# Attention scores of two maps as three 64-row products, one map in each half of the PE rows

## The chip, the cores and the metric

The kernel runs on one core of a Trainium2 chip. The metric is the device time of one execution in microseconds; lower is better. It is compared with the kernel before, run on the same chip.

## What is computed

One layer of an encoder on 1024 tokens of width 1024 in float32: a half-step SwiGLU feed-forward, a mixer, a second half-step feed-forward, each followed by a residual sum and a LayerNorm. Only the mixer is touched. It has two groups of heads:

```
differential attention, 4 heads, two maps m per head, head width 64:
  s[m] = q[m] . k[m] * scale + alibi         128 queries x 1024 keys at a time
  a    = softmax(s[0]) - lam * softmax(s[1]);   o = rms_norm(a . v)
neighbourhood attention, 8 heads of width 64, taken two at a time:
  s    = q . k * scale + bias                128 queries x a window of 264 to 384 keys
  o    = softmax(s) . v
```

So everywhere there are two score maps side by side (two maps of a head, or two heads), each a product over 64 numbers.

## The kernel before

Products are made in a float32 replacement: every operand is split in a rounded part "hi" and a remainder "lo" (fp32r), and a product is a sum of hi.hi, hi.lo and lo.hi.

`project` (L579) makes K and Q of one group of heads from the layer's input: for each half of the tokens 24 matmuls for K (L593 to L595), a split of the sum in PSUM into hi and lo (L606 on ACT, L607 on DVE), then 24 matmuls and a split for Q (L618 ACT, L619 DVE). It is a generator: each step issues three matmuls, and the attention code calls `fill()` at chosen places, which makes a step or two for the next group of heads. These matmuls fill PE while others wait.

The sum in PSUM has map 0 in partitions 0 to 63 and map 1 in 64 to 127. Before, each map gets a tile slice of all 128 partitions: `K[:, j]` holds hi of map j in that map's own half of the partitions and lo in the other half, so L606 and L607 are run once per map on 64 partitions. `Q[:, j, 0]` holds hi of map j in both halves, `Q[:, j, 1]` lo in both; the second half is made by a DMA (L620). One 128-row matmul with Q hi then gives hi.hi + hi.lo, one with Q lo gives lo.hi + lo.lo: two matmuls per map and piece of keys.

`df_scores` (L677) serves 32 units (4 heads, 8 query blocks). For map 1, then map 0: 4 matmuls of 512 columns (L688) into one PSUM tile of `psA` (two slots), a DVE pass that adds the ALiBi table and finds the row minimum (L691), an exponential on ACT (L694). `df_rest` transposes the result (L706), splits it (L708 ACT, L709 DVE) and for every second unit multiplies with V (L715); the tail of that (L724 to L738) goes through ACT, POOL and PE again.

`na_scores` (L814) serves 32 units (4 pairs of heads, 2 row halves, 4 column groups): both heads' scores lie in one `psA` tile, one PSUM bank each. For each head j: 2 matmuls (L825), a DVE pass (L829), an exponential (L831). Then transposes (L850), copies (L851, L852), and the product with V (L858), in which head j writes PSUM partitions 64j to 64j + 63 only, so that the array is used in column halves of 64.

What sets the order on each engine is not the source text: the framework plans a list schedule at compile time. An instruction that the plan finds ready early may go ahead of others that stand before it in the text, and the order on an engine is then fixed. So a unit's score matmuls come out in one or several pieces with other matmuls between them.

Of the kernel before, what the change touches and what calls it, by code (L numbers as in the profile page):

```python
# [9 lines left out]
FT = mybir.dt.float32  # L10
FR = mybir.dt.float32r
FH = mybir.dt.float16
BF = mybir.dt.bfloat16
AF = mybir.ActivationFunctionType
OP = mybir.AluOpType
# [6 lines left out]
P = 128  # L22
S = 1024
# [21 lines left out]
def tile_hybrid_layer(ctx: ExitStack, tc: tile.TileContext, I: dict, out: bass.AP, dbg=None):  # L45
    nc = tc.nc
    V, A, G, T = nc.vector, nc.scalar, nc.gpsimd, nc.tensor
    dma = nc.sync.dma_start
# [4 lines left out]
    psA = ctx.enter_context(tc.tile_pool(name="psA", bufs=2, space=PSUM))  # L53
# [14 lines left out]
    def split_w(src, pool=wsp, tag="wsp", eng=G):  # L68
        st = wst.tile([P, 1024], FT, name="wst")
        dma(st, src)  # L70
        sp = pool.tile([P, 2, 1024], FR, name=tag)
        split(sp[:, 0], sp[:, 1], st, eng)
        return sp
# [9 lines left out]
    def xk(t, k):  # L83
        x = xq[t][k // 4]
        return x[:, 0, k % 4], x[:, 1, k % 4]
# [460 lines left out]
    with ExitStack() as es:  # L546
# [4 lines left out]
        for i in range(2):  # L551
            for tb in range(8):
                o = slice(tb % 4 * P, tb % 4 * P + P)
                ps = psB.tile([P, 512], FT, name="psB")
                terms = []
                for k in range(KT):
                    w, cs = wv[i][k // 2], slice(k % 2 * 512, k % 2 * 512 + 512)
                    hi, lo = xk(tb // 4, k)
# [13 lines left out]
    with ExitStack() as es:  # L572
        kp = es.enter_context(tc.tile_pool(name="kp", bufs=2))
        qp = es.enter_context(tc.tile_pool(name="qp", bufs=3))
# [4 lines left out]
        def project(g):  # L579

            h, na = g["h"], g["kind"] == "na"
            cq, ck = (h, 4 + h) if na else (12 + h, 16 + h)
            scale = -0.125 if na else -0.125 / SLOPES[h]
            wk, wq = (split_w(I["w_in"][c]) for c in (ck, cq))
            K = g["K"] = kp.tile([P, 2, S], FR, name="K")
            g["Q"] = []

            def mm(w, t):
                ps = psB.tile([P, 512], FT, name="psB")
                for k in range(KT):  # L590
                    hi, lo = w[:, 0, k * P:(k + 1) * P], w[:, 1, k * P:(k + 1) * P]
                    xh, xl = xk(t, k)
                    T.matmul(ps, hi, xh, start=k == 0, stop=False)  # L593
                    T.matmul(ps, hi, xl, start=False, stop=False)  # L594
                    T.matmul(ps, lo, xh, start=False, stop=k == KT - 1)  # L595
                    if k < KT - 1:
                        yield ps
                yield ps

            for t in range(2):  # L600
                ts = slice(t * 512, (t + 1) * 512)
                for ps in mm(wk, t):
                    yield
                for j in range(2):
                    a, b = slice(64 * j, 64 * j + 64), slice(64 - 64 * j, 128 - 64 * j)
                    A.activation(K[a, j, ts], ps[a], AF.Copy, scale=scale)  # L606
                    V.scalar_tensor_tensor(K[b, j, ts], ps[a], scale, K[a, j, ts].bitcast(FT), OP.mult, OP.subtract)  # L607
                Q = qp.tile([P, 2, 2, 512], FR, name="Q")
                g["Q"].append(Q)
                for ps in mm(wq, t):  # L610
                    yield
                for j in range(2):
                    a, b = slice(64 * j, 64 * j + 64), slice(64 - 64 * j, 128 - 64 * j)
                    qi, hi, lo = ps[a], Q[a, j, 0], Q[a, j, 1]
                    if na:
                        qi = qi.rearrange("p (r c w) -> p c r w", c=4, w=16)
                        hi, lo = (x.rearrange("p (c r w) -> p c r w", c=4, w=16) for x in (hi, lo))
                    A.copy(hi, qi)  # L618
                    V.tensor_tensor(lo, qi, hi.bitcast(FT), OP.subtract)  # L619
                    dma(Q[b, j].bitcast(FT), Q[a, j].bitcast(FT))  # L620

        PIECES = 32
        groups = [dict(kind="df", h=h) for h in range(4)] + [dict(kind="na", h=h) for h in range(4)]
# [1 line left out]
        def filler(i, places):  # L625
            return Filler(project(groups[i]) if i < 8 else nothing(), PIECES, places)

        for _ in project(groups[0]):
            pass
# [33 lines left out]
        with ExitStack() as e2:  # L663
# [13 lines left out]
            def df_scores(g, qb):  # L677
                slope = SLOPES[g["h"]]
                Q, qo = g["Q"][qb // 4], (qb % 4) * P
                st = sm.tile([P, 8], FT, name="st")  # L680
                mn, bi, z, rz = st[:, 0:2], st[:, 2:4], st[:, 4:6], st[:, 6:8]
                off = 896 - qb * P
                e = [None, None]
                for j in (1, 0):
                    ps = psA.tile([P, S], FT, name="psA")
                    for kc in range(2):
                        for i in range(2):
                            T.matmul(ps[:, kc * 512:(kc + 1) * 512], Q[:, j, i, qo:qo + P],  # L688
                                     g["K"][:, j, kc * 512:(kc + 1) * 512], start=i == 0, stop=i == 1)
                    ej = e[j] = ep.tile([P, S], FT, name="e")  # L690
                    V.tensor_tensor_reduce(ej, ps, dist[:, off:off + S], 1.0, 3e38, OP.add, OP.min,  # L691
                                           accum_out=mn[:, j:j + 1])
                    V.tensor_scalar(bi[:, j:j + 1], mn[:, j:j + 1], slope, None, OP.mult)
                    A.activation(ej, ej, AF.Exp, bias=bi[:, j:j + 1], scale=-slope,  # L694
                                 accum_out=z[:, j:j + 1])
                V.reciprocal(rz, z)
                V.scalar_tensor_tensor(rz[:, 1:2], z[:, 0:1], nlam, rz[:, 1:2], OP.mult, OP.mult)
                V.scalar_tensor_tensor(e[0], e[1], rz[:, 1:2], e[0], OP.mult, OP.add)
                return e[0], rz[:, 0:1]
# [59 lines left out]
            for i, (g, qb) in enumerate(units):  # L759
                if qb == 0 and i:  # L760
                    fill.drain()
                    fill = filler(i // 8 + 1, 24)
                queue.append((g, qb, df_scores(g, qb)))
                if tail:
                    tail.pop()()
                fill()
                if qb == 0:
                    load_v(g)
                if len(queue) > 1:
                    df_rest()  # L770
# [11 lines left out]
        with ExitStack() as e2:  # L782
# [31 lines left out]
            def na_scores(g, r, c, tabs):  # L814
                (r0, nr), (c0, nc_, kind) = NA_R[r], NA_C[c]
                nk = nr * nc_
                t0 = nr * sum(x[0] for x in NA_KINDS[:kind])
                Kg = g["K"].rearrange("p m (r c) -> p m r c", c=GW)
                ps = psA.tile([P, 2, 512], FT, name="psA")
                st = sm.tile([P, 8], FT, name="st")  # L820
                mn, z, rz = st[:, 0:2], st[:, 2:4], st[:, 4:6]
                es_ = []
                for j in range(2):
                    for i in range(2):
                        T.matmul(ps[:, j, 0:nk], g["Q"][r][:, j, i, c * P:(c + 1) * P],  # L825
                                 Kg[:, j, r0:r0 + nr, c0:c0 + nc_], start=i == 0, stop=i == 1)
                    e = pp.tile([P, 384], FT, name="pe")
                    es_.append(e)
                    V.tensor_tensor_reduce(e[:, 0:nk], ps[:, j, 0:nk], tabs[j][:, t0:t0 + nk],  # L829
                                           1.0, 3e38, OP.add, OP.min, accum_out=mn[:, j:j + 1])  # L830
                    A.activation(e[:, 0:nk], e[:, 0:nk], AF.Exp, bias=mn[:, j:j + 1], scale=-1.0,  # L831
                                 accum_out=z[:, j:j + 1])
                V.reciprocal(rz, z)
                for j in range(2):
                    G.tensor_scalar(es_[j][:, 0:nk], es_[j][:, 0:nk], rz[:, j:j + 1], ones, OP.mult, OP.mult)
                return es_
# [58 lines left out]
            for i in range(4, 8):  # L895
                g = groups[i]
# [133 lines left out]
```

## Time and profile before

| | us |
|---|---|
| median of 3 runs (lowest, highest) | 1953.94 (1952.79, 1955.36) |
| the profiled execution | 1954.6 |
| span of its instructions | 1952.8 |
| its part outside the span | 1.8 |
| mixer, differential heads, from 775 to 1013 us | 238 |
| mixer, neighbourhood heads, from 1013 to 1190 us | 177 |

The views name engines as PE (TensorE matmuls), PEld (its weight loads), DVE, ACT, POOL and SP. A matmul's duration contains its way through the array, so that neighbours overlap; what one costs in a row of them is the distance from start to start.

### The profile page before, as it was taken

To read this page: it belongs to the slowest core of one execution; us is meant where nothing else is said; L and a number is where in the kernel's file an instruction comes from. 1 tells how busy PE (TensorE), PEld (TensorE's weight loads), DVE (VectorE), ACT (ScalarE), POOL (GpSimd) and SP (SyncE) were. 2 spreads that over 40 slices of the span, in tenths; PEclk is the share of its full clock that TensorE was granted. 3 is DMA by queue.
4 is the path that set the end of the run, shared out by engine and by line. 5 is a ranking of instruction groups with operands and counts; after the bars stand their busy time and mean duration, and the time that the engine had idled before them with its cause. 6 is when DMAs were issued, how large, how long until landed. Compare 5 with 4: busy or idle time off the path is not lost. (4 is left out here: it accounts for less than half of the span.)

```text
span 1952.8 us, 24037 instructions
## 1 busy us (share of the span) xinstructions
PE 1911.4 (98%) x9056; PEld 1549.9 (79%) x9056; DVE 1205.7 (62%) x1807; ACT 752.5 (39%) x1196; POOL 211.4 (11%) x188
## 2 busy tenths in 40 slices
PE   9999999999999999999999998999999999999998
PEld 7777888878888888788887776887777888878887
DVE  8575656546556811888875455787666555555557
ACT  5333333335332222566655454133333333344331
POOL 0000000000001330011116443100000000000005
PEclk9999999999999999999999999999999999999999
DMA  4656322248762263122123336124554222378632
GB/s 169 217 198 225 119 103 114 108 163 314 250 194 98 103 209 94 43 62 70 47 52 79 90 114 218 74 88 162 195 204 183 102 83 101 134 281 286 194 119 86
DMA packets 109843, 280.41 MB, mean 144 GB/s; under 512 B 12320, under 2 KB 31648, under 8 KB 102048
## 3 DMA queue, kind: packets, MB, share of 16 engines
q1 hardware_dynamic: 109728, 278.89, 41.7%
q8 instruction: 71, 1.16, 0.2%
q14 instruction: 44, 0.36, 0.1%
HBM read 191.29 MB, written 79.17 MB: 138 GB/s over the span
## 5 line engine op out<-in xcount | busy, mean ns | idle before, releaser
L79 PE MATMUL psA<-s,wsp 128*128 128x512 f32 x480 | 189.6, 395 | 0.0
L79 PE MATMUL psA<-x,wsp 128*128 128x512 f32 x448 | 180.7, 403 | 7.7 <-ACT t L378 5.9
L81 PE MATMUL psA<-s,wsp 128*128 128x512 f32 x480 | 187.4, 390 | 0.0
L80 PE MATMUL psA<-s,wsp 128*128 128x512 f32 x480 | 186.7, 389 | 0.0
L65 ACT CAST wsp<-wr 128x1024 fp32r<-128x1024 f32 x124 | 128.9, 1049 | 128.4 <-DVE wr L206 121.3
L80 PE MATMUL psA<-x,wsp 128*128 128x512 f32 x448 | 175.7, 392 | 0.8 <-DVE x L66 0.6
L81 PE MATMUL psA<-x,wsp 128*128 128x512 f32 x448 | 174.9, 390 | 0.0
L66 DVE TENSOR_TENSOR wsp<-wr,wsp 128x1024 fp32r<-128x1024 f32 x124 | 149.4, 1222 | 12.1 <-ACT wsp L65 12.1
L66 DVE TENSOR_TENSOR hd<-wst,hd 128x1024 fp32r<-128x1024 f32 x84 | 101.9, 1224 | 76.3 <-ACT hd L65 73.0
L66 POOL TENSOR_TENSOR wsp<-wst,wsp 128x1024 fp32r<-128x1024 f32 x24 | 60.8, 2538 | 774.2 <-ACT wsp L65 774.2
L205 DVE TENSOR_TENSOR wr<-wr 128x1024 f32<-128x1024 f32 x40 | 49.0, 1224 | 148.5 <-DMA wr<-in_wgu 148.3
L65 ACT CAST hd<-wst 128x1024 fp32r<-128x1024 f32 x84 | 87.7, 1053 | 124.6 <-PE psA L435 31.6
L65 ACT CAST wsp<-wst 128x1024 fp32r<-128x1024 f32 (+1 forms) x86 | 88.7, 1032 | 97.7 <-DMA wst<-wTd 20.7
L79 PEld LDWEIGHTS psA<-x,wsp 128*128 128x128 f32 x448 | 84.0, 187 | 44.0 <-ACT t L378 17.3
L435 PE MATMUL psA<-hd 128*128 128x512 f32 x504 | 116.2, 389 | 0.0
L66 DVE TENSOR_TENSOR wsp<-wst,wsp 128x1024 fp32r<-128x1024 f32 (+1 forms) x62 | 73.6, 1190 | 63.4 <-ACT wsp L65 57.6
L145 POOL TENSOR_TENSOR mv<-mv,cols 128x1 f32<-128x1 f32 x24 | 35.5, 1479 | 712.9 <-DVE mv L144 712.9
L79 PEld LDWEIGHTS psA<-s,wsp 128*128 128x128 f32 x480 | 90.0, 188 | 25.4 <-ACT sg L395 8.2
L435 PEld LDWEIGHTS psA<-hd 128*128 128x128 f32 x504 | 94.6, 188 | 19.6
L593 PE MATMUL psB<-x,wsp 128*128 128x512 f32 x256 | 107.1, 418 | 0.0
L81 PEld LDWEIGHTS psA<-s,wsp 128*128 128x128 f32 x480 | 90.1, 188 | 19.7
L80 PEld LDWEIGHTS psA<-s,wsp 128*128 128x128 f32 x480 | 90.2, 188 | 17.9
(185 smaller groups left out, 4231.0 us busy)
## 6 DMA issues: line engine op xcount, KB each, us to landing
wr<-in_wgu SPq DMA_DIRECT2D x42, 1024.0 KB
hSd<-hs SPq DMA_DIRECT2D x18, 1792.0 KB
wst<-hSd SPq DMA_DIRECT2D x126, 256.0 KB
wst<-wTd SPq DMA_DIRECT2D x72, 256.0 KB
wst<-in_wd SPq DMA_DIRECT2D x54, 256.0 KB
wt<-in_wd SPq DMA_DIRECT2D x18, 512.0 KB
wt<-in_wd SPq DMA_DIRECT2D x36, 256.0 KB
wTd<-wt SPq DMA_DIRECT2D x36, 256.0 KB
```

Of the source, the lines that this page charges most:

```text
L65: A.copy(hi, x)
L66: eng.tensor_tensor(lo, x, hi.bitcast(FT), OP.subtract)
L79: T.matmul(ps, ah, bh, start=start and j == 0, stop=False, skip_group_check=skip)
L80: T.matmul(ps, ah, bl, start=False, stop=False, skip_group_check=skip)
L81: T.matmul(ps, al, bh, start=False, stop=j == n - 1, skip_group_check=skip)
L145: G.tensor_tensor(mv[:, 3:4], mv[:, 2:3], mhalf[:, 0:1], OP.pow)
L205: V.tensor_tensor(l[:, 0:4:3], l[:, 2:4], l[:, 3:5], OP.subtract)
L435: T.matmul(banks[T_], o[:, x, a], o[:, w, 512:1024], start=start and p == 0 and j == 0, stop=p == NP - 1 and j == 2, skip_group_check=not ...
L593: T.matmul(ps, hi, xh, start=k == 0, stop=False)
```

## The change

K and Q are kept once, each map in its own half of the partitions, hi and lo beside each other. The splits run on all 128 partitions at once, the DMA that doubled Q is gone, and lo.lo is left out. A score is three matmuls of 64 rows (hi.hi, hi.lo, lo.hi); those of map 0 and map 1 are issued in turns, with operands in partitions 0 to 63 and 64 to 127. In `df_scores` both PSUM tiles are taken first and all 12 matmuls stand ahead of the first DVE pass; in `na_scores` all 6 stand ahead of it.

```diff
-                for j in range(2):
-                    a, b = slice(64 * j, 64 * j + 64), slice(64 - 64 * j, 128 - 64 * j)
-                    A.activation(K[a, j, ts], ps[a], AF.Copy, scale=scale)
-                    V.scalar_tensor_tensor(K[b, j, ts], ps[a], scale, K[a, j, ts].bitcast(FT), OP.mult, OP.subtract)
-                Q = qp.tile([P, 2, 2, 512], FR, name="Q")
+                A.activation(K[:, 0, ts], ps, AF.Copy, scale=scale)
+                V.scalar_tensor_tensor(K[:, 1, ts], ps, scale, K[:, 0, ts].bitcast(FT), OP.mult, OP.subtract)
+                Q = qp.tile([P, 2, 512], FR, name="Q")
...
-                    A.copy(hi, qi)
-                    V.tensor_tensor(lo, qi, hi.bitcast(FT), OP.subtract)
-                    dma(Q[b, j].bitcast(FT), Q[a, j].bitcast(FT))
+                A.copy(hi, qi)
+                V.tensor_tensor(lo, qi, hi.bitcast(FT), OP.subtract)
...
+                pss = [psA.tile([P, S], FT, name="psA") for _ in range(2)]
+                for kc in range(2):
+                    for i, (x, y) in enumerate(((0, 0), (0, 1), (1, 0))):
+                        for j in range(2):
+                            a = slice(64 * j, 64 * j + 64)
+                            T.matmul(pss[j][:, kc * 512:(kc + 1) * 512], Q[a, x, qo:qo + P],
+                                     g["K"][a, y, kc * 512:(kc + 1) * 512], start=i == 0, stop=i == 2)
                 for j in (1, 0):
-                    ps = psA.tile([P, S], FT, name="psA")
-                    for kc in range(2):
-                        for i in range(2):
-                            T.matmul(ps[:, kc * 512:(kc + 1) * 512], Q[:, j, i, qo:qo + P],
-                                     g["K"][:, j, kc * 512:(kc + 1) * 512], start=i == 0, stop=i == 1)
+                    ps = pss[j]
...
+                for i, (x, y) in enumerate(((0, 0), (0, 1), (1, 0))):
+                    for j in range(2):
+                        a = slice(64 * j, 64 * j + 64)
+                        T.matmul(ps[:, j, 0:nk], g["Q"][r][a, x, c * P:(c + 1) * P],
+                                 Kg[a, y, r0:r0 + nr, c0:c0 + nc_], start=i == 0, stop=i == 2)
                 for j in range(2):
-                    for i in range(2):
-                        T.matmul(ps[:, j, 0:nk], g["Q"][r][:, j, i, c * P:(c + 1) * P],
-                                 Kg[:, j, r0:r0 + nr, c0:c0 + nc_], start=i == 0, stop=i == 1)
```

## Rows read from the trace of the kernel before

**Rows 1.** The page, part 1: busy time, share of the span, instructions.
```profile
PE 1911.4 (98%) x9056; PEld 1549.9 (79%) x9056; DVE 1205.7 (62%) x1807; ACT 752.5 (39%) x1196; POOL 211.4 (11%) x188
```
**Rows 2.** Busy time by stage: stretch, its length, engines in the columns' order PE, PEld, DVE, ACT, POOL.
```profile
775.00:1013.00 238.00, 229.43 (x1300) 190.57 (x1299) 199.24 (x430) 149.97 (x297) 31.63 (x23) 1.00 0.20 55
1013.00:1190.00 177.00, 166.50 (x1032) 127.48 (x1033) 91.56 (x284) 96.64 (x265) 89.22 (x115) 0.97 0.35 97
```
**Rows 3.** Groups by line, 700 to 1340 us: the score matmuls (busy, mean ns | idle before).
```profile
L688 PE MATMUL psA<-K,Q 128*128 128x512 f32 x256 | 72.1, 399 | 0.4 <-DVE st L691 0.4
L825 PE MATMUL psA<-K,Q 128*128 128x384 f32 (+3 forms) x128 | 34.8, 358 | 6.2 <-DVE st L829 6.1
```
**Rows 4.** Timeline of PE, one differential unit: start us, length us.
```profile
802.20 1.98 PE L688 MATMUL psA<-K,Q 128*128 128x512 f32 x8
804.01 0.39 PE L593 MATMUL psB<-x,wsp 128*128 128x512 f32 x1
```
**Rows 5.** Timelines of PE and DVE, one neighbourhood unit.
```profile
1088.11 0.42 PE L825 MATMUL psA<-K,Q 128*128 128x288 f32 x2
1088.36 0.39 PE L593 MATMUL psB<-x,wsp 128*128 128x512 f32 x1
...
1088.83 0.40 PE L595 MATMUL psB<-x,wsp 128*128 128x512 f32 x1
1089.19 0.53 PE L825 MATMUL psA<-K,Q 128*128 128x288 f32 x2
1089.57 0.39 PE L593 MATMUL psB<-x,wsp 128*128 128x512 f32 x1
...
1089.06 0.08 DVE L829 DVE_READ_ACCUMULATOR2_ANT st<- 128x1 f32 x1
```
**Rows 6.** Waits from 1013 to 1190 us: total us, times, longest.
```profile
PEld psA L825 <- DVE st L829: 13.5, 22, 3.2
...
PE psA L825 <- DVE st L829: 6.1, 5, 2.7
```
**Rows 7.** Timelines of PE and PEld around one product with V in column halves.
```profile
1054.84 0.40 PE L595 MATMUL psB<-x,wsp 128*128 128x512 f32 x1
1055.16 1.15 PE L858 MATMUL psB<-PT,Vc 128*64 128x128 f32 x12
...
1056.04 0.27 PE L858 MATMUL psB<-PT,Vc 96*64 96x128 f32 x1
1056.24 0.50 PE L593 MATMUL psB<-x,wsp 128*128 128x512 f32 x1
1056.58 0.40 PE L594 MATMUL psB<-x,wsp 128*128 128x512 f32 x1
...
1056.24 0.19 PEld L593 LDWEIGHTS psB<-x,wsp 128*128 128x128 f32 x1 [0.17 <-issue]
```
**Rows 8.** PE's L858 matmuls begun up to two instants of that product (stretch, busy, count).
```profile
1055.10:1055.44 0.34, 0.27 (x3) 1.00 0.30 76
1055.10:1055.82 0.72, 0.65 (x9) 1.00 0.30 75
```
**Rows 9.** Timeline of PE: first and last piece of L688 (71) and of L825 (61).
```profile
775.76 1.98 PE L688 MATMUL psA<-K,Q 128*128 128x512 f32 x8
...
1011.40 0.63 PE L688 MATMUL psA<-K,Q 128*128 128x512 f32 x2
1011.87 1.47 PE L715 MATMUL psB<-aT,Vt 128*128 128x256 f32 x11
1013.17 0.41 PE L825 MATMUL psA<-K,Q 128*128 128x264 f32 x2
...
1183.55 0.54 PE L825 MATMUL psA<-K,Q 128*128 128x288 f32 x2
```
**Rows 10.** Groups by line, 700 to 1340 us: splits of 64 and of 128 partitions.
```profile
L709 DVE TENSOR_TENSOR aT<-psB,aT 128x512 fp32r<-128x512 f32 x64 | 43.3, 685 | 3.2 <-ACT aT L708 3.0
...
L708 ACT CAST aT<-psB 128x512 fp32r<-128x512 f32 x64 | 35.5, 584 | 19.3 <-PE psB L706 18.9
...
L607 DVE SCALAR_TENSOR_TENSOR K<-psB,K 64x512 fp32r<-64x512 f32 x32 | 22.0, 688 | 51.0 <-ACT K L606 50.3
...
L606 ACT ACTIVATE K<-psB 64x512 fp32r<-64x512 f32 x32 | 18.9, 589 | 20.4 <-PE psB L595 10.9 <-DVE K L607 9.1
```

## Prediction before the run

> **What bounds the kernel now.** I read the page's busy shares first: PE is busy 98% of the span and no other engine over 62% [rows 1]. A share of the whole says little about the stage that is changed, so the windows by stage come next: with the differential heads PE is busy 229.4 of 238 us and DVE 199.2; with the neighbourhood heads PE 166.5 of 177 and DVE only 91.6 [rows 2]. PE ends both stages: its idle time is 8.6 and 10.5 us, and its order is fixed, so a microsecond more or less of PE work moves the end by nearly as much. The granted clock is 1.00 and 0.97 there, so PE time can be read at the upper level. The groups by line give the size of what is changed: 256 score matmuls of 512 columns and 128 of 264 to 384 (mean 322) [rows 3]. Their mean durations overlap; the price comes from the timeline: eight L688 from 802.20 to the next matmul at 804.01 are 0.227 us each [rows 4], and two L825 of 288 columns take 0.25 [rows 5], 0.125 each, or some 0.14 at 322.
>
> **The change, part by part.** One execution is the base: 1954.6 us, of which 1952.8 are span; the median of the runs is 1953.94, 0.7 less. About 0.2% (4 us) is what a measurement of this kernel can tell from no change.
>
> *Matmuls.* A differential unit had 8 and gets 12 of half the rows. The trace has no matmul of 64 rows. It does have halves of the array's columns, in L858: three of them start in the first stretch of a product, before the second head joins, then six within 0.38 us [rows 8], 63 ns each, although within one column half they follow each other at 109 ns (of the twelve the last three start between 1055.82 and 1056.04, two such distances [rows 7, 8]). So two halves of the array do work at once in this kernel. For row halves the bounds are 0.227 us per pair (both at once) and 0.454 (one after the other). I take 0.227, as the row of the nearest kind shows overlap. Six pairs replace eight matmuls: 2 x 0.227 x 32 units = 14.5 us less. A neighbourhood unit goes from 4 to 3 slots: 32 x 0.14 = 4.5 us less.
>
> *Entering and leaving the halves.* This is the price that decides, and again L858 is the nearest row. From L595 to the first L858 it is 0.325 us instead of 0.227: 0.10 lost, and the weight load that usually hides behind a matmul starts only then. On the way out the last L858 starts at 1056.04 and would be followed 0.109 later; L593 comes at 1056.24, its weight load marked with 0.17 us in which it waited for nothing visible, and L594 follows after 0.34 instead of 0.227 [rows 7]. So out is 0.09 of emptying plus 0.11 of exposed load; in is 0.10 plus the same 0.11 for a 128-column load. One visit costs 0.41 us, near the 0.454 that a unit saves. Bounds: 0 (row halves switch freely) and 0.41; I take 0.41, since all the trace's changes between whole array and halves pay it. The Trainium skill (TensorEngine Tiling (Array Packing), Key Properties) says that changing the tiling mode, not merely the tile, drains TensorE. The trace agrees for column halves with the 0.17 us above; no run here shows it for row halves. By that rule the sum is the one below; without it the first rival's.
>
> *How many visits.* The plan breaks a unit's scores in pieces: L688 stands in 71 pieces for 32 units, from one of eight to one of two with L715 behind it; L825 in 61 [rows 9]. For the differential heads I take two per unit, 64, with ends at 32 (each unit in one piece) and 85 (longer lists are broken more). 64 x 0.41 = 26.2 us. A piece with an odd count leaves one half empty for a slot: half of the pieces x 0.114 = 3.6 us. Differential heads: -14.5 + 26.2 + 3.6 = +15.3.
>
> For the neighbourhood heads the two pieces per unit have a cause: the second L825 pair starts at 1089.19, right after DVE has read the first head's scores at 1089.14 [rows 5]; they share a tile. Waits of L825 for that read are 13.5 us on the load side and 6.1 on the matmul side [rows 6]. The change puts all six matmuls ahead of the read, so this wait goes; I take 7 us, between 3 (the 2.7 and 2.2 us stalls are those of a late bias table and of the last heads without filler, and may return at the transposes) and 10. With the cause gone I expect 1.25 pieces per unit, 40 visits (ends 32 and 61): 16.4 us. 18 of the 122 borders of L825 pieces lie against L858, which already pays one border: 18 x 0.2 = 3.6 less. Odd pieces 0.6. Neighbourhood heads: -4.5 - 7 + 16.4 - 3.6 + 0.6 = +1.9.
>
> *Splits, DMAs and passes.* A split costs the same on 64 and 128 partitions (688 and 685 ns on DVE, 589 and 584 on ACT) [rows 10], so half of 64 go on each: 22 us off DVE, 19 off ACT, over eight groups of heads. 32 DMAs of 256 KB leave SP's queue, with nothing moved past it. All of that lies beside PE's filler matmuls; what it can give is a part of PE's 8.6 us idle time. I take 1 us, between 0 and 4. The DVE pass of map 1 now stands behind all 12 matmuls instead of 4, some 0.5 to 1 us later; its readers come an iteration later and PE has other matmuls meanwhile: nothing. If that cover were gone, as with the last unit of a stage, 1 us once. The first matmul needs both PSUM slots instead of one; in steady units they are free when the scores come, and where not, the plan puts filler first: inside the count of pieces.
>
> **Sum.** +15.3 + 1.9 - 1 = +16.2: 1954.6 + 16.2 = 1970.8, said as 1971. This case alone reaches from 32 + 32 visits with the larger wait and no odd pieces (-1.4 - 5.0 - 3 = about -9: 1946) to 85 + 61 visits with the smaller wait (+25.2 + 15.0 = +40: 1995).
>
> **Rivals.**
> 1. *Row halves switch freely.* Its place is the border between L595 and L688, its price 0 instead of 0.41; it decides below some 0.2 us per visit, where the sum changes sign. Then -14.5 + 3.6 with the differential heads, -4.5 - 7 + 0.6 with the others, -1: -23, 1932. For it: row halves leave the way to PSUM as wide as it was, other than column halves. Against it: the border costs of L858 are the same whatever stands beside it. 16%.
> 2. *The halves take turns.* Pairs at 0.454 us: with the differential heads 128 x 0.227 = +29 instead of -14.5, and visits +26.2; with the others 64 x 0.14 = +9 instead of -4.5, waits and visits as above +5.8; -1: +69, odd pieces costing nothing here: 2024. It decides as soon as a pair takes over 0.3 us. For it: no row shows row halves at work; against it: column halves overlap [rows 8]. The Trainium skill (TensorE: Matmul & The Clock Gate, Part 3) reports four row tiles at 3.07 times the speed of one after the other; no run here shows that. 12%.
> 3. *The plan keeps each unit in one piece.* 32 + 32 visits: differential -14.5 + 13.1 = -1.4, neighbourhood -4.5 - 7 + 13.1 - 3.6 = -2, -1: about -4 to -9, 1948. For it: the differential lists are longer, so that PE is fuller in the plan; against it: 71 pieces now. 9%.
> 4. *Nothing measurable*, where PE's idle time takes up what the visits add: 5%. Against it: the idle time lies at other places.
>
> **How the numbers follow.** My case has 58%. Its middle is slower; of its spread some 0.05 falls within 4 us and 0.02 below. Faster: 0.16 + 0.08 of rival 3 + 0.02 = 0.26, with a little of rival 4 0.27. Same: 0.05 + 0.04 = 0.09. Slower: the rest of mine and rival 2, 0.64. The range goes from 1930, so that most of rival 1 is in, to 2000, the end of mine and a little; outside lie rival 2 and an edge of rival 1, under 2 in 10. My own case's range is 1946 to 1995.
>
> **What would show it.** In the timeline after: starts of the two halves' matmuls in pairs a few ns apart, and 0.22 to 0.24 us from pair to pair (rival 2: 0.45). From L595 to the first score matmul 0.32 or more, and a score piece followed by a weight load with about 0.17 us of unexplained idle time; rival 1 has neither. The pieces of L688's successor counted: some 64, and 40 with the neighbourhood heads. The wait of the scores for L829 gone. The stage from 775 grows by about 15 us, the next by 2. I am wrong if the first stage shrinks, or if PE's busy time there grows while its end stays.

## The result, and the profile after

The kernel after takes 1984.9 us (median of five runs, 1977.17 to 1986.13) against 1953.94 before: 1.0144 times the time, with an interval of 1.0127 to 1.016. That is 31 us more, inside the range and on the side that was forecast, but nearly twice the 16.2 us of the sum. The profiled execution took 1985.38 us, 1983.6 of it span.

The page's busy shares say little, as before [rows 1]: PE gained 23 us of busy time and the span 31.

```profile
PE 1934.2 (98%) x9248; PEld 1542.1 (78%) x9248; DVE 1184.7 (60%) x1775; ACT 731.3 (37%) x1164; POOL 209.2 (11%) x188
```

The windows by stage show where the time went (columns as in [rows 2]). The stage from 775 us to the first neighbourhood scores now ends at 1054 instead of 1013, with 21.9 us in which PE is idle instead of 8.6, and at a mean clock of 0.98; the next one is 9 us shorter.

```profile
775.00:1054.00 279.00, 257.10 (x1465) 191.98 (x1464) 197.49 (x427) 144.47 (x291) 31.91 (x24) 0.98 0.11 34
1054.00:1222.00 168.00, 161.05 (x1042) 117.26 (x1041) 72.50 (x257) 81.25 (x240) 86.99 (x113) 0.95 0.25 73
```

Work of the two stages overlaps at their border, so from here on I cut at the last tail transposes of the differential heads (L735, before L737), and call what lies from the first score matmul to there the differential stage, and from there to the last product with V the neighbourhood stage. By that cut, in one profiled execution of each kernel, the change adds 34.5 us to the first (252.6 to 287.1) and takes 3.4 from the second (164.3 to 160.9). The rest of the program is unchanged.

The groups by line (700 to 1360 us) stand beside [rows 3] and [rows 10]: 384 score matmuls of 64 rows in place of 256, 192 in place of 128, and a split that takes 0.69 us on 128 partitions as it did on 64. The scores' wait for the DVE pass fell from 6.1 us to 2.4.

```profile
L684 PE MATMUL psA<-K,Q 64*128 64x512 f32 x384 | 69.3, 421 | 0.0
L824 PE MATMUL psA<-K,Q 64*128 64x264 f32 (+3 forms) x192 | 26.9, 368 | 2.6 <-DVE st L829 2.4
L605 DVE SCALAR_TENSOR_TENSOR K<-psB,K 128x512 fp32r<-128x512 f32 x16 | 11.0, 689 | 50.0 <-ACT K L604 50.0
```

What had grown is in the waits from 775 to 1054 us (total us, times, longest). On the matmul side the tail transposes L735 wait 15.8 us for the end of their chain, where the corresponding wait of before (L737, from 775 to 1013 us, the second view) is 4.4 in five. On the load side there is a row that stands for the visits themselves: the first score load of a piece waits, 32 times, for nothing visible, and so does L593 behind a piece, 17 times.

```profile
PEld psB L735 <- issue: 20.9, 13, 3.5
PE psB L735 <- DVE rr L730: 15.8, 11, 3.1
...
PEld psA L684 <- issue: 8.9, 32, 0.4
...
PEld psB L593 <- issue: 6.2, 17, 0.4
PE psB L704 <- DVE e L696: 5.0, 9, 1.0
```

```profile
PE psB L737 <- DVE rr L732: 4.4, 5, 0.9
```

One of the long tail waits, on PE (timeline: start, length). Twelve score matmuls end near 885, and the next instruction in PE's order is the tail's transpose, 3.06 us later.

```profile
883.06 0.40 PE L595 MATMUL psB<-x,wsp 128*128 128x512 f32 x1
883.39 1.65 PE L684 MATMUL psA<-K,Q 64*128 64x512 f32 x12
888.10 0.66 PE L735 MATMUL psB<-ident,rr 128*128 128x128 f32 x2 [3.06 <-DVE rr L730]
888.41 0.77 PE L593 MATMUL psB<-x,wsp 128*128 128x512 f32 x1
888.98 0.63 PE L594 MATMUL psB<-x,wsp 128*128 128x512 f32 x1
```

Behind the wait the first two filler matmuls stand 0.57 us apart (888.41 to 888.98); behind another tail of the same trace, at full speed, it is 0.32 (868.54 to 868.86). The windows show why: the granted clock is 1.00 up to 887 and 0.51, the 1.2 GHz level, for the next 7 us. Two more of the three long waits (near 957 and 1028 us) are followed by such stretches. From 775 to 1217 us the time at the lower level adds up to 30.7 us after and 13.6 before; a microsecond of PE work costs two there. Of the 30.7 us after, 13.7 lie in the differential stage and 17.0 in the other, near 1075 and 1206 us.

```profile
880.00:887.00 7.00, 5.04 (x37) 3.83 (x35) 4.42 (x5) 3.28 (x9) 2.35 (x1) 1.00 0.00 0
887.00:894.00 7.00, 5.90 (x22) 4.59 (x24) 4.42 (x11) 2.80 (x5) 0.69 (x1) 0.51 0.32 94
```

### The profile page after: what moved, and what is told of

The parts are those of the page before. It is cut to its first block, busy times and chain, and to the rows that moved or that the text cites. A ratio compares the mean times of both kernels' runs of the same rounds, so it can differ in the third digit from the quotient of the medians.

```text
span 1983.6 us, 24174 instructions
## 1 busy us (share of the span) xinstructions
PE 1934.2 (98%) x9248; PEld 1542.1 (78%) x9248; DVE 1184.7 (60%) x1775; ACT 731.3 (37%) x1164; POOL 209.2 (11%) x188
## 5 line engine op out<-in xcount | busy, mean ns | idle before, releaser
L65 ACT CAST wsp<-wr 128x1024 fp32r<-128x1024 f32 x124 | 129.0, 1050 | 128.3 <-DVE wr L206 121.4
L66 DVE TENSOR_TENSOR wsp<-wr,wsp 128x1024 fp32r<-128x1024 f32 x124 | 149.4, 1223 | 12.0 <-ACT wsp L65 12.0
L66 DVE TENSOR_TENSOR hd<-wst,hd 128x1024 fp32r<-128x1024 f32 x84 | 101.9, 1223 | 76.5 <-ACT hd L65 73.2
L66 POOL TENSOR_TENSOR wsp<-wst,wsp 128x1024 fp32r<-128x1024 f32 x24 | 57.8, 2410 | 805.8 <-ACT wsp L65 805.7
L65 ACT CAST hd<-wst 128x1024 fp32r<-128x1024 f32 x84 | 87.8, 1054 | 124.6 <-PE psA L435 28.8
L65 ACT CAST wsp<-wst 128x1024 fp32r<-128x1024 f32 (+1 forms) x86 | 88.8, 1033 | 99.5 <-PE psB L435 20.0
L593 PE MATMUL psB<-x,wsp 128*128 128x512 f32 x256 | 113.3, 443 | 0.0
L66 DVE TENSOR_TENSOR wsp<-wst,wsp 128x1024 fp32r<-128x1024 f32 (+1 forms) x62 | 73.8, 1190 | 62.7 <-ACT wsp L65 58.3
```

The costliest lines, as they stand in the source:

```text
L65: A.copy(hi, x)
L66: eng.tensor_tensor(lo, x, hi.bitcast(FT), OP.subtract)
```

## The experiments

The theory after the traces: the half rows do what the sum said (work in pairs, a fixed price per visit), and two things were not in it, the new order of the matmuls and the tail waits. The rival: the price of a visit is larger than 0.41 us and explains all.

### What a visit costs, by itself

In place of the layer (which is left out, the output is the input) a row of matmuls: six of the whole array, then some in halves, again and again.

> This kernel leaves the whole layer out: its output is the input, and it only runs rows of matmuls of one kind behind each other, so that their prices can be read from start to start. Theory (each visit to row halves is paid on the way in and out, the halves work at once): a pair of 64-row matmuls 0.23 us in a long row; a visit of six pairs between whole matmuls 6 x 0.23 + 0.41 us; a visit of one pair 0.23 + 0.41; a visit of a single 64-row matmul the same as that of one pair; a long row in one half alone 0.23 each. Rival (halves switch freely and the loss after the change came from the plan): a visit of six pairs 1.4 us, of one pair 0.25. For six matmuls in one half and then six in the other I have no firm number: between 1.4 us (the queue reaches past six) and 2.8 us plus the visit.

Timeline of PE of that kernel: six whole ones and a visit of six pairs; of one pair (L77); long rows of 64 in turns and of 32 in one half; six in one half and then six in the other (L91); six halves of 288 columns (L96) and four whole ones (L101).

```profile
36.98 1.65 PE L70 MATMUL full<-w 128*128 128x512 f32 x6
38.57 1.66 PE L72 MATMUL h<-w 64*128 64x512 f32 x12
40.16 1.65 PE L70 MATMUL full<-w 128*128 128x512 f32 x6
...
61.19 1.66 PE L75 MATMUL full<-w 128*128 128x512 f32 x6
62.78 0.51 PE L77 MATMUL h<-w 64*128 64x512 f32 x2
...
106.72 7.79 PE L83 MATMUL h<-w 64*128 64x512 f32 x64
114.35 7.41 PE L85 MATMUL h<-w 64*128 64x512 f32 x32
121.69 1.65 PE L88 MATMUL full<-w 128*128 128x512 f32 x6
123.28 2.23 PE L91 MATMUL h<-w 64*128 64x512 f32 x12
125.44 1.65 PE L88 MATMUL full<-w 128*128 128x512 f32 x6
...
153.79 1.66 PE L94 MATMUL full<-w 128*128 128x512 f32 x6
155.38 0.66 PE L96 MATMUL h<-w 64*128 64x288 f32 x6
155.97 0.51 PE L94 MATMUL full<-w 128*128 128x512 f32 x1
...
188.74 0.69 PE L101 MATMUL h<-w 128*128 128x288 f32 x4
189.27 1.54 PE L99 MATMUL full<-w 128*128 128x512 f32 x6
```

A whole matmul costs 0.230 us from start to start. The long row in turns takes 114.35 - 106.72 = 7.63 us for 32 pairs, 0.238 each; the row in one half 7.34 us for 32 matmuls, 0.229 each. So two halves do nearly twice the work of one: rival 2 is out. A round of six whole ones and six pairs takes 40.16 - 36.98 = 3.18 us; without 6 x 0.230 and 6 x 0.238 there remain 0.37 us for going in and out, and the mean of twelve rounds gives 0.36. With one pair the rounds take 2.01 us on average, which leaves 0.39; with a single half matmul 1.99 us, which leaves 0.38. So rival 1 is out as well. The load of the first half matmul is where it shows (weight loads, same kernel):

```profile
25.89 1.23 PEld L72 LDWEIGHTS h<-w 64*128 64x128 f32 x12 [0.36 <-issue]
```

The Trainium skill (TensorEngine Tiling (Array Packing), Key Properties) says that a change of the tiling mode drains TensorE; this run agrees for row halves, with 0.36 to 0.39 us for there and back.

A differential unit in one piece is then 3.18 - 1.38 = 1.80 us against 8 x 0.230 = 1.84 before: a gain of 0.04 us in the best case, and a loss of 0.36 or more with each further piece. Six halves of 288 columns with their visit take 155.97 - 153.79 - 1.38 = 0.80 us against 189.27 - 188.74 = 0.53 for four whole ones: by these prices a neighbourhood unit can't gain at all. And the order inside a unit counts: six in one half and then six in the other (L91) need 125.44 - 121.69 - 1.38 = 2.37 us, 0.57 more than in turns.

### The order alone, and each kind of head alone

`orders` keeps the whole-row matmuls of before and takes only the new order; `na_order` does that in the neighbourhood heads alone.

```diff
 # both: all four matmuls of na_scores ahead of the first DVE pass
                 for j in range(2):
                     for i in range(2):
                         T.matmul(ps[:, j, 0:nk], ...
+                for j in range(2):
...
 # orders alone, in df_scores
+                pss = [psA.tile([P, S], FT, name="psA") for _ in range(2)]
+                for kc in range(2):
+                    for i in range(2):
+                        for j in range(2):
+                            T.matmul(pss[j][:, kc * 512:(kc + 1) * 512], Q[:, j, i, qo:qo + P], ...
                 for j in (1, 0):
-                    ps = psA.tile([P, S], FT, name="psA")
...
+                    ps = pss[j]
```

`df_new` makes the whole change for the differential heads only, `na_new` for the neighbourhood heads only (each chooses the splits and the scores by the kind of the group).

> The kernel before with its whole-row matmuls, layouts and DMAs, but in the order of the changed kernel: both PSUM tiles first and all score matmuls of a unit ahead of the first DVE pass, in both kinds of heads. Theory (the loss is the visits and what follows from them): the differential heads stay within 4 us, the neighbourhood heads lose their wait for the DVE pass, so 1954 - 8 = 1946 (1942 to 1951). Rival (the order itself makes the loss, by the plan and its waits): differential heads 15 us or more longer, 1965 or more.

> Only the differential heads changed (half-row products and their layouts); neighbourhood heads as before. Theory: this carries the loss, 1978 to 1988, since the accounts of the two traces put some 30 us on these heads and little on the others. Rival (the loss comes from both, or from what the heads do to each other): 1965 to 1975.

> Only the neighbourhood heads changed, differential heads as before. Theory: saved matmuls and the wait that goes are about the 38 visits: 1954 within 4 us. Rival (the visits are dear here too): 1960 or more. Rival (visits are free, the loss is one of the differential heads alone): 1944 or less.

> The kernel before with one edit: in the neighbourhood heads the four whole-row matmuls of a unit stand ahead of the first DVE pass. Theory (the order gains there and costs with the differential heads): the 13 us that the last stage lost in the run with both orders changed come through alone, 1941 (1937 to 1946). Rival (the two stages only traded filler with each other, so that neither gains by itself): 1950 to 1956.

| kernel | median us | ratio to before [interval] | differential stage, us | neighbourhood stage, us |
|---|---|---|---|---|
| before | 1953.94 | | 252.6 | 164.3 |
| after | 1984.9 | 1.0144 [1.0127, 1.016] | 287.1 | 160.9 |
| orders | 1952.66 | 0.9992 [0.9982, 1.0001] | 264.8 | 151.4 |
| df_new | 1988.6 | 1.0177 [1.0164, 1.019] | 284.8 | 161.4 |
| na_new | 1949.57 | 0.9985 [0.997, 1.0] | 256.3 | 157.6 |
| na_order | 1941.76 | 0.9945 [0.9933, 0.9957] | 252.7 | 152.4 |

`orders` was a miss, and the most useful run: its whole comes out even, but only because two effects cancel. The order costs the differential heads 12.2 us and gives the neighbourhood heads 12.9. So of the 34.5 us that the change adds to the differential stage 12.2 come from the order and 22.3 from the half rows with their layouts; and its 3.4 us in the other stage are 12.9 from the order less 9.5 for the half rows. The priced rounds would make that last term 32 x (0.80 - 0.53) = 8.6. `na_new` gives a smaller loss (12.9 - 6.7 = 6.2), so these parts are known to a few microseconds only: each kernel has its own plan, and each stage time is that of one execution. `df_new` lies just above the range of its theory, `na_new` just below; the ten executions of `na_new` spread over 15.5 us.

Two things limit this account. The clock differs between the executions: `orders` and `after_wdve` (below) both spend 6.8 us of the neighbourhood stage at the lower level, the kernel after 17.0. `after_wdve` has the neighbourhood scores of the kernel after and takes 155.9 us there, 4.5 more than `orders`; so about half of the 9.5 us is clock, and the half rows themselves cost these heads some 4.5, near the priced 8.6 less the 3.6 that the prediction put down for borders which L858 pays already. And the parts need not add up: half rows in the old order were not run.

What the order does to the differential heads is in the waits of `orders` from 775 to 980 us: its transposes (L708) wait for the exponentials, since the first DVE pass starts later: 4.5 us after a unit's first score matmul on average, where it is 2.7 before.

```profile
PEld psB L708 <- issue: 7.4, 5, 2.5
PE psB L708 <- DVE e L700: 4.2, 6, 2.2
PE psB L708 <- DVE st L695: 3.5, 2, 1.8
```

In the same stretch of the kernel before the corresponding rows are small:

```profile
PE psB L706 <- DVE e L698: 1.7, 2, 1.5
PEld psB L706 <- issue: 1.1, 3, 0.5
```

Over the whole stage PE's waits before the transposes are 9.9 us in `orders` (to 1036 us) and 1.7 before, but only 5.0 + 1.0 = 6.0 in the kernel after. So the order's cost at this place isn't the same in the two kernels.

In the neighbourhood heads the order is all gain: `na_order` took 1941.76 us, as its theory had it. In it the four matmuls of a unit stand together (timeline), and the waits from 1013 to 1180 us that stood at 13.5 and 6.1 us [rows 6] are down to 3.2 and 2.5; the pieces of L825 fall from 61 to 36. With the waits goes time at the lower clock, 13.6 us in this stage before and 6.8 in `na_order`. It is faster than both kernels of this case.

```profile
1088.46 0.88 PE L825 MATMUL psA<-K,Q 128*128 128x384 f32 x4
```

```profile
PEld psA L825 <- DVE st L830: 3.2, 2, 2.9
PE psA L825 <- DVE st L830: 2.5, 1, 2.5
```

### The tail later, and the halves one after the other

`after_tail` calls the tail's last step behind the next unit's transposes; `no_turns` issues the six matmuls of map 1 and then those of map 0; `best` is the kernel before with the order of `na_order` and the later tail.

```diff
 # after_tail, best
-                if tail:
-                    tail.pop()()
+                late = tail.pop() if tail else None
...
+                if late:
+                    late()
 # no_turns
-                for kc in range(2):
-                    for i, (x, y) in enumerate(((0, 0), (0, 1), (1, 0))):
-                        for j in range(2):
+                for j in (1, 0):
+                    for kc in range(2):
+                        for i, (x, y) in enumerate(((0, 0), (0, 1), (1, 0))):
```

> The changed kernel with one edit: the two transposes that end a differential unit pair, with the sum and the store behind them, are called after the next unit's transposes instead of straight after its scores. Theory (the plan puts PE in front of these two before their chain over ACT, DVE and POOL is done, since half-row scores pass faster than planned): most of the 18 us of waits before them go, and a part of the clock's low stretches: 1972 (1966 to 1977). Rival (the wait only moves to the next thing that PE needs): 1981 to 1988.

> The changed kernel with one edit: in the differential heads the six half-row matmuls of map 1 stand before the six of map 0 instead of in turns. Theory (halves work at once only as far as the queue reaches past the first half's matmuls; the single prices gave 2.36 us for such a visit against 1.79 in turns): 32 x 0.57 = 18 us more than the changed kernel, 2003 (1997 to 2010). Rival (what bounds these units is not the matmuls but the waits, or DVE gains from map 1 being done early): 1980 to 1992.

> The kernel before with whole-row products, the neighbourhood heads' four matmuls ahead of the DVE pass and the late transposes of the run beside this one. Theory: 13 us for the first and up to 7 of the 10 us of waits before those transposes: 1935 (1930 to 1942). Rival (with whole rows the plan already has filler before them, so that nothing is left to gain): the same as with the first edit alone.

`after_tail` took 1977.53 us, 1.0125 [1.0106, 1.0143]: between the two expectations, with an interval that overlaps that of the kernel after, so that the gain in the whole isn't clear of noise. The trace shows the exchange. PE's time lost ahead of the tail transposes (what the start-to-start distances there have beyond the matmul's own) falls from 18.7 us to 3.5 over the mixer, but some 9 us come back at the scores, which now wait for the DVE pass that frees their PSUM tile (waits from 775 us on):

```profile
PE psA L684 <- DVE st L689: 5.0, 8, 0.7
```

In the trace after, the matmul side has no such row. The tail wait had partly hidden a second limit.

`no_turns` took 1971.94 us, 1.0095 [1.0078, 1.0113], 13 us less than the kernel after where I had expected 18 more, and below the range of the rival too. A unit does pay the price: twelve matmuls now take 2.16 us to the next start, against 1.58 in turns (803.22 to 804.80 in the trace after) and 1.81 for eight before [rows 4].

```profile
819.07 2.22 PE L684 MATMUL psA<-K,Q 64*128 64x512 f32 x12
821.23 0.50 PE L593 MATMUL psB<-x,wsp 128*128 128x512 f32 x1
```

But the plan leaves these units whole: 37 pieces in place of 59, 22 x 0.38 = 8 us less, and the time lost ahead of the tails is 8.6 instead of 18.7. PE is busy longer under the same chain, so it waits less for it. What the rival named shows as well: with map 1 done early, DVE's first pass starts 2.5 us after a unit's first score matmul (4.3 in the kernel after), and PE's waits before the transposes fall from 6.0 us to 1.2.

`best` took 1946.25 us, 0.9963 [0.995, 0.9975], more than `na_order` alone and outside both expectations: with the matmuls of before the tail stood well where it was.

### What the long tail waits wait for

One chain of a tail, the one of the timeline above, in the timelines of ACT, POOL and DVE after (start, length, idle time before it):

```profile
883.44 1.04 ACT L65 CAST wsp<-wst 128x1024 fp32r<-128x1024 f32 x1
884.38 0.37 ACT L725 ACTIVATE oT<-psB,st 128x128 f32<-128x128 f32 x1
...
884.56 2.35 POOL L66 TENSOR_TENSOR wsp<-wst,wsp 128x1024 fp32r<-128x1024 f32 x1 [16.52 <-ACT wsp L65]
887.07 0.69 POOL L728 TENSOR_TENSOR rr<-rr,cols 128x2 f32<-128x2 f32 x1 [0.17 <-DVE rr L727]
...
884.87 2.06 DVE L727 TENSOR_SCALAR rr<-rr 128x2 f32<-128x2 f32 x1 [0.97 <-ACT oT L725]
887.80 0.23 DVE L730 TENSOR_TENSOR rr<-rr,st 128x1 f32<-128x1 f32 x2 [0.87 <-POOL rr L728]
```

The split of the next head's weights stands inside the chain: its rounding on ACT (L65, 1.04 us) between the two squares, its subtraction on POOL (L66, 2.35 us) ahead of L728. And the 128x2 operation L727, which takes 0.17 us in thirteen of sixteen chains, takes 2.06 us here, until POOL's operation ends. All three long chains have this form. Two edits: `after_act` makes L727 on ACT (with `before_act` and `na_order_act` as the same edit in the kernels before and `na_order`), `after_wdve` makes L66 of these weights on DVE.

```diff
 # after_act, before_act, na_order_act
-                V.tensor_scalar(rr[:, 2:4], rr[:, 0:2], 1.0 / P, EPS, OP.mult, OP.add)
+                A.activation(rr[:, 2:4], rr[:, 0:2], AF.Copy, scale=1.0 / P, bias=EPS)
 # after_wdve
-            wk, wq = (split_w(I["w_in"][c]) for c in (ck, cq))
+            wk, wq = (split_w(I["w_in"][c], eng=V) for c in (ck, cq))
```

> The changed kernel, with one small operation moved: the 128x2 scale-and-add of L727 in each tail chain goes from DVE to ACT. In the changed kernel's trace it takes 0.17 us 13 times and 2.06 us three times, each time until POOL's 128x1024 split (L66) ends; a wait of PE of some 3 us and a stretch at the lower clock level follow each of the three (6.8, 3.4 and 3.4 us long). Theory: DVE is held there by POOL, and this is a part of what the half rows cost. Then the three holds go (3 x 1.9 = 5.7 us), and with them the low stretches behind them (half of 13.6 = 6.8 us): 1972 to 1979 us, waits of the tail transposes for L730 under 11 us (from 15.8). Rival: PE comes to the tail early in any case and waits for another link of the chain; 1982 to 1987 us.

> The kernel before, with the same operation moved to ACT. There one of 16 was held, by 0.66 us, and no low stretch of the differential heads follows it: 1951 to 1956 us by both theories. If it gains 4 us or more, the operation on DVE costs something in any kernel and the run before it says nothing about the half rows.

> The kernel before with the neighbourhood heads' four whole-row matmuls ahead of the first DVE pass (the fastest so far, 1942 us) and the same operation moved to ACT: 1939 to 1944 us, the gain of the order unchanged.

> The changed kernel, with the lo part of the K and Q weights (L66, 128x1024) made by DVE instead of POOL. In the changed kernel three of the sixteen tail chains find POOL inside that operation for 2.35 us, and PE then waits 3.1 us; moving L727 to ACT left these three waits at 2.8 us, since L728 then stood behind the same operation in POOL's queue. Theory: that operation inside the chain is the cause of the three long waits and of the low clock behind two or three of them. Then the three waits fall by some 2 us each and the low stretches (half of 13.6 us) go: 1972 to 1979 us. Rival: DVE's own operation of 1.2 us, or the score passes behind it, takes the place: 1981 to 1988 us.

`after_act` took 1983.18 us, 1.0145 [1.013, 1.0161]: no gain, the rival's answer. L727 now takes 0.20 us, but L728 starts only when POOL is through with L66 (timeline of POOL), and PE still waits 2.76 us.

```profile
884.09 2.35 POOL L66 TENSOR_TENSOR wsp<-wst,wsp 128x1024 fp32r<-128x1024 f32 x1 [16.46 <-ACT wsp L65]
886.39 0.69 POOL L728 TENSOR_TENSOR rr<-rr,cols 128x2 f32<-128x2 f32 x1
```

`before_act` took 1952.62 us, 0.9988 [0.9979, 0.9997], and `na_order_act` 1940.8, 0.993 [0.9918, 0.9943]: both as expected, 2 and 1 us less than the kernels without the edit (1954.72 in the same comparison, and 1941.76).

`after_wdve` took 1974.72 us, 1.0099 [1.0083, 1.0115], 10 us less than the kernel after and in the range of the theory. The same wait (timeline of PE) is down to 1.97 us, where the theory had it some 2 us shorter, and the stretch that had run at 0.51 is at 1.00:

```profile
889.27 0.40 PE L735 MATMUL psB<-ident,rr 128*128 128x128 f32 x2 [1.97 <-DVE rr L730]
```

```profile
887.00:894.00 7.00, 5.03 (x34) 3.58 (x31) 5.30 (x13) 3.24 (x7) 0.69 (x1) 1.00 0.28 95
```

The three waits give about 3 x 1.1 = 3.3 us. Time at the lower level falls from 30.7 to 6.8 us over the same stretch, at half speed worth up to 12.0. Together that is more than the 10 us, so the new plan lost some elsewhere. Not all of it is the tails: by the stage cut 6.5 us of the gain lie in the differential stage (287.1 to 280.6) and 5.0 in the other (160.9 to 155.9). There 10.2 us at the lower level, near 1206 us, are gone, and why the clock stayed up in `after_wdve` isn't shown. So the number of the theory came in part from a place that it did not speak of.

## Why the prediction was right, and where it was not

- **Pairs, right where the plan leaves them in turns.** Taken at 0.227 us, measured at 0.238: 32 x (6 x 0.238 - 8 x 0.227) = -12.4 instead of -14.5.
- **"A piece with an odd count leaves one half empty", mis-sized.** The plan did more than leave odd counts: in the trace after seven pieces of six hold one half alone and last as long as twelve in turns. Of all 384 score matmuls 80 start with no other within 30 ns. At 0.119 us each that is up to 9.5 us instead of 3.6. One such piece (timeline of PE after; twelve in turns took 1.65 us at 883.39):

```profile
783.60 1.66 PE L684 MATMUL psA<-K,Q 64*128 64x512 f32 x6
```

- **The price of a visit, right.** 0.41 was read off column halves; row halves cost 0.36 to 0.39.
- **Pieces, right.** 64 and 40 were predicted, 59 and 38 came. 59 x 0.38 = 22.4 us against 26.2.
- **"The DVE pass of map 1 now stands behind all 12 matmuls ... nothing", wrong.** This is the step that failed. The prediction let the pass come 0.5 to 1 us later and named the filler as cover. In `orders` it comes 1.8 us later, and the differential stage is 12.2 us longer, because the transposes behind it then wait for the exponentials.
- **Not in the sum: the tails.** With the new order but whole rows PE loses 6.6 us ahead of the tail transposes, after the change 18.7. That is 12 us, and with -12.4 + 22.4 it makes the 22 of the differential half rows. That this closes is luck. Not in it are the matmuls without a partner (up to 9.5 us) and the time at the lower clock in this stage (13.7 us against 3.4 in `orders`, worth up to 5); the other way, the waits before the transposes are shorter (6.0 against 9.9), and eleven of the 59 pieces end at a tail's wait, which covers their way out. So how the 22 divide is known only roughly. Three chains that contain the weight split make the worst of it, and the time at the lower clock behind them; moving one operation gave 10 us back, 6.5 of them in this stage. I had written that PE's order is fixed, so that PE work moves the end, and did not ask which chain on another engine would be late once PE's own work between two of its waits was shorter: twelve in turns take 1.58 us to the next start where eight took 1.81. That PE's twelve matmuls are shorter than the plan counts is my reading of why the tail stands so close behind them; `no_turns`, where they take longer and the wait shrinks, speaks for it, but the plan's costs were not tried.
- **"this wait goes; I take 7 us", mis-sized.** The order gave the neighbourhood heads 11.9 (`na_order`) to 12.9 us (`orders`), above even the bound of 10: each wait also broke the unit in two, and up to 3.4 us are the time at the lower clock that went with the waits. The half rows cost them 9.5 where the sum had -4.5 + 16.4 - 3.6 + 0.6 = +8.9; that these agree is luck, since about half of the 9.5 is clock.
- **"I take 1 us" for less work in the splits: not seen.** DVE and ACT are 21 us less busy each, as worked out, and no gain of the whole can be laid to that.

The predicted +16.2 and the measured 31 differ by 14.8: +12.2 for the order in the differential heads, +7.0 for their half rows (22.3 against 15.3), -5.9 for the order in the others, +0.6 for their half rows, +1 for the splits. So the side was forecast for a reason that holds, visits that cost more than the pairs save, but that the time lies in the range is in part luck: the range reached up to 1995 for more pieces, and what came instead were the order, the tails and matmuls without a partner.

Of the signs, the pairs (152 in the differential heads, a few ns apart), the 0.33 us from L595 to the first score matmul (883.06 to 883.39) and the counts of pieces came; so did the idle time before the load behind a piece, with 0.36 us on average (6.2 in 17) instead of 0.17. The scores' wait for L829 shrank without going (2.4 us), and the stages grew by 34.5 and -3.4 us instead of 15 and 2. Two small terms are not derived in the prediction: 0.6 for odd pieces with the neighbourhood heads, where half of 40 pieces at 0.07 would be 1.4, and the -3 in its lower bound, where the splits were bounded at 4.

## What to carry to other kernels

Row halves of the array pay only in long stays: here a visit costs as much as 1.6 matmuls of 512 columns, so that a saving of two per unit is nearly eaten by the first visit and lost with the second, and a compile-time plan that mixes units makes more visits (59 for 32 units). When a change moves several things, run its order without its arithmetic, and read the granted clock of each stage before comparing stage times; two effects of 12 us with opposite signs looked like nothing, and the useful half was worth keeping alone (`na_order`, 0.9945 of the time before). When work on the bounding engine gets shorter, look for the chain over other engines that it used to cover.

## What was not expected of the hardware

- Six matmuls in one row half followed by six in the other take 2.37 us with their visit, less than 12 x 0.229 + 0.36 = 3.1 and more than 1.80 in turns: the second six overlap the first in part, without being issued in turns. The third and the fourth to start stand 7 ns apart (123.845 and 123.852 us), where matmuls of one half stand 0.229 us apart, so one of the second half starts ahead of some of the first.
- A 128x2 fp32 scale-and-add on DVE took 2.06 us instead of 0.17, ending within 0.03 us of POOL's 128x1024 subtraction, three times of three in the trace after. In the trace before, one of the three that lay beside such a POOL operation took 0.83 us. DVE's operations that read PSUM and lay beside one took no longer in the trace after: five 128x512 subtractions (L707, 0.68 us) and four 128x1024 passes (L689, 1.22 us); nor did two 128x1 operations (L691, 0.15 us). The Trainium skill (Advanced Engine Details and Errata, Mode Summary) says that DVE's second SBUF port is shared with GpSimd and that its two-port modes and GpSimd block each other; the trace agrees, though it doesn't show in which mode L727 ran.
- After each of the three waits of some 3.1 us PE ran at the 1.2 GHz level for 3 to 7 us; after those of 1.97 us in `after_wdve` it did not. In `after_act` all three were 2.8 us long, and the first was followed by full speed, the second by a stretch at the lower level (windows of `after_act`):

```profile
887.00:894.00 7.00, 6.67 (x39) 5.11 (x40) 5.88 (x16) 3.34 (x6) 0.09 (x1) 1.00 0.29 94
...
958.60:962.00 3.40, 3.40 (x17) 2.27 (x15) 2.08 (x8) 2.94 (x6) 0.00 (x0) 0.59 0.12 40
```

The length of the wait alone doesn't decide. In `no_turns` PE waited only 1.50 and 1.51 us before two of these transposes (903.21 and 972.66 us), and 6.8 and 3.4 us at the lower level followed; behind a third wait of 1.69 us the clock stayed up. The first of these stretches (windows of `no_turns`):

```profile
903.20:910.00 6.80, 6.79 (x19) 4.76 (x20) 5.45 (x10) 3.26 (x6) 0.00 (x0) 0.50 0.23 83
```

So such a wait can cost twice, once while it lasts and once in what follows. The five executions of the kernel after, which spread over 9 us, roughly follow their mean clock: 1977.17 us at 0.995, 1979.34 at 0.994, 1985.38 and 1986.13 at 0.991, 1984.9 at 0.989. The kernel before spreads too, over 7.9 us in the 23 executions beside `orders`.
